# Part of a vector-matrix product moved from TensorE to ScalarE and GpSimd in a decoder layer

## The chip, the cores and the metric

The kernel runs on one core of a Trainium2 chip. The metric is the device time of one execution in microseconds (us), lower is better. Five engines work side by side, each in its own order: TensorE (PE; PEld is its weight load), VectorE (DVE), ScalarE (ACT), GpSimd (POOL) and SyncE (SP), which issues the transfers. [...]

## The reference

One post-norm decoder layer with D = 2048 and 1024 tokens. What matters here is its first part and one factor of its last:

```python
mod = c @ w_ada + b_ada                      # c (1, 2048), w_ada (2048, 6144)
shift, scale, gate = jnp.split(mod, 3, axis=-1)
h = _ln(x) * (1.0 + scale[:, None, :]) + shift[:, None, :]
proj = h @ w_in                              # (1024, 2048) by (2048, 9776), then the two mixers
...                                          # y: both mixers, merged and projected
x = _ln(ALPHA * x + gate[:, None, :] * y) * ln_g + ln_b
```

So `c @ w_ada` is a product of one vector with a matrix of 48 MB in float32; it has to be read once, and each weight is used once. Scale and shift are needed ahead of everything, the gate only at the end.

## The kernel before

A planner orders the instructions: the program is written in the order of the computation, and a timeline that the compiler works out ahead of the run fixes each engine's order. At run time an engine takes its instructions in that order and waits where one is not ready.

**First stage: scale and shift, and the first projection tiles.** x is loaded, normalised and transposed into 16 tiles xs[k] of 128 channels by 1024 tokens. Then the loop over k = 0, 2, ... 14 (eight rounds) makes scale and shift for two k at a time. In each round eight tiles wa of w_ss are loaded (512 KB each, `load_wa`, L150; they rotate through seven buffers, four of the pool p0 and three of the pool st, whose tag "stg" other stages share). A tile holds two chunks of 128 input channels by 512 columns. L187 multiplies each chunk on TensorE by the matching chunk of c, held in cP as 128x32 with c in the first column and zeros beside it. The 32 output rows of a chunk go to one of four groups of PSUM partitions of the bank mp, so four chunks are wanted at a time, and the bank sums over the loads. One float32 matmul shows as two rows in the trace, so one load as four. Then ScalarE copies mp to pm (L189), four matmuls with a column of ones sum over the partitions (L191), and VectorE adds the bias (L192, L193). With them VectorE scales and shifts xs[k] (L199), ScalarE rounds it (hhi, L201), VectorE takes the rest (hlo, L203), and `mm6` (L124, L125, L128) multiplies three projection tiles with three matmuls for each half of the tokens, 36 for two k. In between VectorE computes the tables of the state-space mixer (`Ssm.tables`, lines L1072 to L1148), which no one needs before the next stage. All loads go through SP's queue in one order.

**Second stage: dense tiles and blocks of the state-space mixer.** `dense` makes one projection tile: four weight units, each loaded (L109), rounded by ScalarE (whi, L111), its rest taken by VectorE (wlo, L113), and multiplied by `mm6`, 24 matmuls for a unit. Eight blocks of the mixer (`Ssm.block`) are laid between, two tiles to a block, three to the first. A block goes from TensorE (L1252 to L1274) to a long chain on VectorE (L1193, L1303) and back to TensorE (L1320, L1321). `gate_steps` is a generator that `dense` calls once for each unit. It computes the gate: for each of four blocks of 512 columns, eight loads wg of 512 KB in the tag "stg" (three buffers, which the evictions of the dense tiles use too), each with four chunks multiplied on TensorE as above (L365); after eight loads two copies by ScalarE (L370, L371), the load of the bias, one matmul with ones (L374) and an addition (L375).

Behind these come attention, the branches and the output projection, none of them touched. GpSimd has two uses in the kernel, both behind the second stage: a mask's addition in attention (L904) and the addition of ln_b in the last norm (L596).

Of the kernel before, what the change touches and what calls it, by code (L numbers as in the profile page):

```python
# [5 lines left out]
F32 = mybir.dt.float32  # L6
# [7 lines left out]
ADD, SUB, MUL, MAX, MIN = ALU.add, ALU.subtract, ALU.mult, ALU.max, ALU.min  # L14
# [16 lines left out]
def hybrid_kernel(tc, A, out):  # L31
    with ExitStack() as es:
        _hybrid(es, tc, A, out)
# [17 lines left out]
def _hybrid(es, tc, A, out):  # L51
    nc = tc.nc
    V, S, P, PE = nc.vector, nc.scalar, nc.gpsimd, nc.tensor
    ld, st_ = nc.sync.dma_start, nc.sync.dma_start
# [32 lines left out]
    cst = es.enter_context(tc.tile_pool(name="cst", bufs=1))  # L87
    ident = cst.tile([128, 128], F32, name="ident")
    ld(ident, A["ident"])
    ones = cst.tile([128, 128], F32, name="ones")  # L90
    V.memset(ones, 1.0)
    bada = cst.tile([128, KT, 2], F32, name="bada")
    ld(bada, A["bada"])
# [4 lines left out]
    stp = es.enter_context(tc.tile_pool(name="st", bufs=3))  # L98
# [5 lines left out]
    def w_unit(src, shape=[128, 4, 128], rp=None):  # L104

        raw = (rp or wp).tile([128, 512], F32, name="wraw", tag="wraw", bufs=3 if rp else WR)
        if len(shape) == 3:
            raw = raw.rearrange("p (k c) -> p k c", k=4)
        ld(raw, src)  # L109
        hi = wp.tile(shape, F32R, name="whi", tag="whi")  # L110
        S.copy(hi, raw)  # L111
        lo = wp.tile(shape, F32R, name="wlo", tag="wlo")
        V.tensor_tensor(lo, raw, f(hi), op=SUB)  # L113
        return hi, lo
# [15 lines left out]
    def stage(dt=F32):  # L130
        return stp.tile([128, T], dt, name="stg", tag="stg")
# [3 lines left out]
    cP = sc.tile([128, KT, 32], F32, name="cP")  # L135
# [5 lines left out]
    p0 = s0.enter_context(tc.tile_pool(name="p0", bufs=1))  # L141
# [2 lines left out]
    NS = 3  # L144
    units = []


    def load_wa(n):
        wa = (stp if n % 7 % 2 else p0).tile([128, 2, 512], F32, name="wa", tag="stg" if n % 7 % 2 else "wa", bufs=3 if n % 7 % 2 else 4)
        ld(wa, A["w_ss"][n // 8][:, 2 * (n % 8):2 * (n % 8) + 2])  # L150
        return wa

    xn, was = [], {}
    for b in range(NB):
        t = xh.tile([128, T], F32, name=f"xa{b}", tag="xh"), xh.tile([128, T], F32, name=f"xb{b}", tag="xh")
# [24 lines left out]

    for k in range(0, KT, 2):
        mp = pp.tile([128, 512], F32, name="mp", tag="mp", bufs=2)
        for n in range(8):
            wa = was.pop(4 * k + n) if 4 * k + n in was else load_wa(4 * k + n)
            for i in range(2):
                r = 32 * (2 * n % 4 + i)
                PE.matmul(mp[r:r + 32], cP[:, 2 * n + i], wa[:, i], start=n < 2, stop=n > 5, tile_position=(0, r))  # L187
        pm = p0.tile([128, 512], F32, name="pm", tag="pm", bufs=1)
        S.copy(pm, mp)  # L189
        for i in range(4):  # L190
            PE.matmul(mp[:, i:i + 1], pm[:, 128 * i:128 * i + 128], ones[:, :1], start=True, stop=True)  # L191
        V.tensor_tensor(mods[:, k:k + 2], mp[:, :4].rearrange("p (k i) -> p k i", k=2), bada[:, k:k + 2], op=ADD)  # L192
        V.tensor_scalar(mods[:, k:k + 2, 0:1], mods[:, k:k + 2, 0:1], 1.0, None, op0=ADD)  # L193
        if k % 4 == 0:
            units.append([w_unit(w_in[TILES["us"][i]][:, k:k + 4]) for i in range(NS)])

    acc = [[pp.tile([128, 512], F32, name="acc", tag="st", bufs=6) for _ in range(2)] for _ in range(NS)]
# [50 lines left out]
    def bank():  # L248
        return pss.tile([128, 512], F32, name="sps", tag="s")
# [103 lines left out]
    def gate_steps():  # L353

        for c in range(4):
            gp = bank()
            for hf in range(2):
                cs = slice(512 * c + 256 * hf, 512 * c + 256 * hf + 256)
                o = gp[:, 256 * hf:256 * hf + 256]
                for u in range(4):  # L360
                    wg = stp.tile([128, 4, 256], F32, name="wg", tag="stg")
                    ld(wg, A["w_gate"][4 * u:4 * u + 4, :, cs].rearrange("k p c -> p k c"))
                    for i in range(4):
                        r = 32 * i
                        PE.matmul(o[r:r + 32], cP[:, 4 * u + i], wg[:, i], start=u == 0, stop=u == 3, tile_position=(0, r))  # L365
                    yield
            cs = slice(512 * c, 512 * c + 512)
            s = stage()
            t, b = s[:, :512], s[0:32, 512:]
            S.copy(t, gp)  # L370
            S.copy(b, gp[0:32])  # L371
            ld(b, A["b_gate"][0:1, cs].to_broadcast([32, 512]))
            g2 = bank()
            PE.matmul(g2[0:32], ones[:, 0:32], t, start=True, stop=True)  # L374
            V.tensor_tensor(b, b, g2[0:32], op=ADD)  # L375
            st_(gate_d[:, cs], b[0:1])

# [25 lines left out]
    sp_cm = tc.tile_pool(name="sp", bufs=1)  # L403
    sp = sp_cm.__enter__()
    side = gate_steps()
    n = 0
    for b in range(8):
# [145 lines left out]
    with (tc.tile_pool(name="at2", bufs=1, side="right") as ap,  # L553
# [3 lines left out]
        def work():  # L557
            for i, t in enumerate(branch_nsa(psum_a, opd, 0)):
                st_(na_d[i], t)
                yield 1  # L560
            yield from glu(psum_a, (opd, opx), ap)
            yield from branch_ssm(psum_a, (opd, opx))

        w, n, grp = work(), 0, None
# [11 lines left out]
    mp = es.enter_context(tc.tile_pool(name="mp", bufs=32, side="right"))  # L576
# [74 lines left out]
    for c in range(4):  # L651
        cs = slice(512 * c, 512 * c + 512)
# [780 lines left out]
```

## Time and profile before

| | us |
|---|---|
| median of 3 runs | 3239.2 (3238.16 to 3239.89) |
| the profiled execution | 3234.84 |
| its span, first to last instruction | 3233.1 |
| TensorE busy | 3162.2 (98%) |
| VectorE busy | 1686.2 (52%) |
| ScalarE busy | 1127.2 (35%) |
| GpSimd busy | 85.5 (3%) |

The profile shows one execution. A window of it lists for each engine how long it was busy and how many instructions it had, the granted clock of TensorE (1.00 is 2.4 GHz) and the share of the DMA engines' time. The chain of waits is the work that ended last, followed back from the end; its shares by line tell which line the end waited for. A line of the timeline begins with an instruction's start and its duration, and in brackets stands how long the engine was idle ahead of it and for what. A busy TensorE need not be at its peak: a lone matmul on a quarter of the array is as busy as a full one.

### The profile page before, as it was taken

Reading aid. Unit: us, or ns where it says so; the run is one execution under the profiler, and the core shown is the slowest. Engines: PE = TensorE matmul, PEld = TensorE weight load, DVE = VectorE, ACT = ScalarE, POOL = GpSimd, SP = SyncE. Lnnn points to the kernel's source line nnn. Section 1 sums busy time; section 2 is a strip of 40 time slices with the busy share of each in tenths; the row PEclk is TensorE's granted clock in tenths of the full one; section 3 lists DMA queues with packets and bytes.
Section 4 is the critical chain, followed back from the end, with each engine's and each line's share of the span. In section 5 each row is a group of like instructions: output and inputs, shape, how many; then the busy total and the mean of one; then the engine's idle time right before and its main releaser. Section 6 shows DMA issues by size and latency. Waiting matters only on the chain.

```text
span 3233.1 us, 43112 instructions
## 1 busy us (share of the span) xinstructions
PE 3162.2 (98%) x15603; PEld 2538.1 (79%) x15603; DVE 1686.2 (52%) x4615; ACT 1127.2 (35%) x2327; POOL 85.5 (3%) x66
## 2 busy tenths in 40 slices
PE   7999999999999999999999999999999999999896
PEld 4467788888888888888888888887888888788784
DVE  8354678763444434334333334426777665534737
ACT  4212222222433334333433234325555443322323
POOL 0000000000000000000000000000000000000302
PEclk9999999999999999999999999999999999999998
DMA  9654524344322232222322222236668444734533
GB/s 335 236 170 147 172 94 141 103 128 119 117 92 74 77 97 88 71 64 83 97 77 74 67 84 91 76 126 202 213 207 285 142 131 147 241 114 144 166 119 138
DMA packets 286398, 432.21 MB, mean 134 GB/s; under 512 B 40324, under 2 KB 139428, under 8 KB 286184
## 3 DMA queue, kind: packets, MB, share of 16 engines
q1 hardware_dynamic: 286184, 429.45, 41.0%
q8 instruction: 123, 2.02, 0.3%
q14 instruction: 91, 0.75, 0.1%
HBM read 331.30 MB, written 98.05 MB: 133 GB/s over the span
## 4 chain that ended last, share of the span: by engine, by line
PE 93%; DVE 3%; DMA 2%; ACT 1%; issue 1%; SPq 0%; ACTq 0%; DVEq 0%
PE dps L124 17%; PE dps L125 17%; PE dps L128 17%; PE po L957 5%; PE ps L814 4%; PE pt L935 4%; PE pa L462 4%; PE pa L463 4%; PE pa L464 4%; PE e L602 2%; PE e L601 2%; PE e L603 2%; PE mp L187 2%; DVE r L595 1%; PE acc L124 1%; PE e L462 1%
## 5 line engine op out<-in xcount | busy, mean ns | idle before, releaser
L124 PE MATMUL dps<-hhi,whi 128*128 128x512 f32 x2336 | 927.8, 397 | 0.0
L125 PE MATMUL dps<-hlo,whi 128*128 128x512 f32 x2336 | 925.2, 396 | 0.0
L128 PE MATMUL dps<-hhi,wlo 128*128 128x512 f32 x2336 | 750.3, 396 | 0.0
L111 ACT CAST whi<-wraw 128x512 fp32r<-128x512 f32 x544 | 336.2, 619 | 1054.9 <-PE dps L125 622.7
L113 DVE TENSOR_TENSOR wlo<-wraw,whi 128x512 fp32r<-128x512 f32 x544 | 381.0, 701 | 600.9 <-ACT whi L111 587.8
L124 PEld LDWEIGHTS dps<-hhi,whi 128*128 128x128 f32 x2336 | 439.7, 188 | 103.8 <-issue 13.0
L125 PEld LDWEIGHTS dps<-hlo,whi 128*128 128x128 f32 x2336 | 439.8, 188 | 93.7 <-issue 7.0
L128 PEld LDWEIGHTS dps<-hhi,wlo 128*128 128x128 f32 x2336 | 433.4, 188 | 92.5 <-issue 5.7
L940 DVE TENSOR_TENSOR ptl<-pt,pth 128x512 fp32r<-128x512 f32 (+2 forms) x320 | 204.1, 646 | 269.3 <-ACT pth L939 267.6
L939 ACT CAST pth<-pt 128x512 fp32r<-128x512 f32 (+2 forms) x320 | 172.0, 552 | 456.7 <-PE pt L935 456.0
L462 PE MATMUL pa<-op,whi 128*128 128x512 f32 x528 | 210.0, 400 | 2.1 <-ACT op L449 1.7
L463 PE MATMUL pa<-op,whi 128*128 128x512 f32 x528 | 209.7, 397 | 2.5 <-DMA op<-oa_d 2.5
L464 PE MATMUL pa<-op,wlo 128*128 128x512 f32 x528 | 208.8, 396 | 0.0
L602 PE MATMUL e<-wlo,m 128*128 128x512 f32 x368 | 148.0, 402 | 9.9 <-DVE rsd L42 5.4
L603 PE MATMUL e<-whi,m 128*128 128x512 f32 x368 | 146.3, 398 | 0.0
L929 ACT ACTIVATE psl<-psl,mn 128x128 f32<-128x128 f32 (+7 forms) x128 | 99.2, 775 | 81.3 <-DVE mn L842 80.5
L601 PE MATMUL e<-whi,m 128*128 128x512 f32 x368 | 122.0, 401 | 0.6 <-ACT whi L111 0.6
L462 PEld LDWEIGHTS pa<-op,whi 128*128 128x128 f32 x528 | 99.8, 189 | 23.3 <-ACT op L449 3.3
L463 PEld LDWEIGHTS pa<-op,whi 128*128 128x128 f32 x528 | 99.6, 189 | 22.9 <-DMA op<-oa_d 2.9
L464 PEld LDWEIGHTS pa<-op,wlo 128*128 128x128 f32 x528 | 99.6, 189 | 20.1 <-issue 0.7
L904 POOL TENSOR_TENSOR near<-bn,msk 128x512 f32<-128x512 f32 x32 | 35.1, 1098 | 2662.1 <-DVE msk L900 2535.9
L883 ACT ACTIVATE pw<-pw,mn 128x640 f32<-128x640 f32 (+4 forms) x128 | 88.9, 694 | 32.4 <-DVE mn L842 31.6
(308 smaller groups left out, 4271.1 us busy)
## 6 DMA issues: line engine op xcount, KB each, us to landing
wraw<-in_w_in SPq DMA_DIRECT2D x304, 256.0 KB, 3.0
wraw<-in_w_out SPq DMA_DIRECT2D x136, 256.0 KB, 3.0
wa<-in_w_ss SPq DMA_DIRECT2D x64, 512.0 KB, 5.7
wg<-in_w_gate SPq DMA_DIRECT2D x32, 512.0 KB, 3.6
q<-q_d SPq DMA_DIRECT2D x64, 256.0 KB, 4.1
wraw<-in_w_bn SPq DMA_DIRECT2D x64, 256.0 KB, 3.1
q_d<-stg SPq DMA_DIRECT2D x32, 256.0 KB, 3.9
oa_d<-ptl SPq DMA_DIRECT2D x64, 128.0 KB, 2.2
```

The costliest lines, as they stand in the source:

```text
L111: S.copy(hi, raw)
L113: V.tensor_tensor(lo, raw, f(hi), op=SUB)
L124: PE.matmul(ps[hf], hi[:, ku], hhi[k][:, c], start=a, stop=False)
L125: PE.matmul(ps[hf], hi[:, ku], hlo[k][:, c], start=False, stop=False)
L128: PE.matmul(ps[hf], lo[:, ku], hhi[k][:, c], start=False, stop=z)
L462: PE.matmul(ps, hi[:, j], x[k][0], start=k == 0, stop=False)
L463: PE.matmul(ps, hi[:, j], x[k][1], start=False, stop=False)
L464: PE.matmul(ps, lo[:, j], x[k][0], start=False, stop=k == 7)
L601: PE.matmul(a, mk[0][:, t], hi, start=k == 0, stop=False)
L602: PE.matmul(a, mk[0][:, t], lo, start=False, stop=False)
L603: PE.matmul(a, mk[1][:, t], hi, start=False, stop=k == KT - 1)
L940: V.tensor_tensor(lo[0:n, :w], tp[0:n, :w], f(hi[0:n, :w]), op=SUB)
```

## The change

In the first stage, of the eight loads of a round the even ones go to TensorE as before, now with the other two groups of partitions for every second one. The odd ones go to ScalarE, which multiplies each chunk, partition by partition, with c as the scale of the instruction (`scaled_sum`, S.mul). The first odd tile of a round is written to an accumulator pa of 128x2x512; each later one is multiplied in place and added to pa by GpSimd (one addition of 128x1024). At the end of a round VectorE adds mp and the two halves of pa into pm, in the place of ScalarE's copy. In the second stage all of the gate's product goes that way: its loads are cut as 2 chunks by 512 columns instead of 4 by 256, ScalarE multiplies, GpSimd adds to gacc and adds the halves, and the one matmul with ones stays. The copy of the bank to SBUF goes, and the tile of ones shrinks.

```diff
-    ones = cst.tile([128, 128], F32, name="ones")
+    ones = cst.tile([128, 32], F32, name="ones")
...
+    def scaled_sum(acc, w, k, first):
+        for i in range(2):
+            S.mul((acc if first else w)[:, i], w[:, i], cP[:, k + i, 0:1])
+        if not first:
+            P.tensor_tensor(acc, acc, w, op=ADD)
...
         mp = pp.tile([128, 512], F32, name="mp", tag="mp", bufs=2)
+        pa = p0.tile([128, 2, 512], F32, name="pacc", tag="pacc", bufs=2)
         for n in range(8):
             wa = was.pop(4 * k + n) if 4 * k + n in was else load_wa(4 * k + n)
-            for i in range(2):
-                r = 32 * (2 * n % 4 + i)
-                PE.matmul(mp[r:r + 32], cP[:, 2 * n + i], wa[:, i], start=n < 2, stop=n > 5, tile_position=(0, r))
-        pm = p0.tile([128, 512], F32, name="pm", tag="pm", bufs=1)
-        S.copy(pm, mp)
+            if n % 2:
+                scaled_sum(pa, wa, 2 * n, n == 1)
+            else:
+                for i in range(2):
+                    r = 32 * (n % 4 + i)
+                    PE.matmul(mp[r:r + 32], cP[:, 2 * n + i], wa[:, i], start=n < 3, stop=n > 3, tile_position=(0, r))
+        pm = pa[:, 0]
+        V.tensor_tensor(pm, mp, pm, op=ADD)
+        V.tensor_tensor(pm, pm, pa[:, 1], op=ADD)
...
     def gate_steps():
         for c in range(4):
-            gp = bank()
-            for hf in range(2):
-                cs = slice(512 * c + 256 * hf, 512 * c + 256 * hf + 256)
-                o = gp[:, 256 * hf:256 * hf + 256]
-                for u in range(4):
-                    wg = stp.tile([128, 4, 256], F32, name="wg", tag="stg")
-                    ld(wg, A["w_gate"][4 * u:4 * u + 4, :, cs].rearrange("k p c -> p k c"))
-                    for i in range(4):
-                        r = 32 * i
-                        PE.matmul(o[r:r + 32], cP[:, 4 * u + i], wg[:, i], start=u == 0, stop=u == 3, tile_position=(0, r))
-                    yield
             cs = slice(512 * c, 512 * c + 512)
-            s = stage()
-            t, b = s[:, :512], s[0:32, 512:]
-            S.copy(t, gp)
-            S.copy(b, gp[0:32])
+            gacc = sp.tile([128, 2, 512], F32, name="gacc", tag="gacc")
+            for u in range(8):
+                wg = stp.tile([128, 2, 512], F32, name="wg", tag="stg")
+                ld(wg, A["w_gate"][2 * u:2 * u + 2, :, cs].rearrange("k p c -> p k c"))
+                scaled_sum(gacc, wg, 2 * u, u == 0)
+                yield
+            P.tensor_tensor(gacc[:, 0], gacc[:, 0], gacc[:, 1], op=ADD)
+            g2 = bank()
+            PE.matmul(g2[0:32], ones, gacc[:, 0], start=True, stop=True)
+            b = stage()[0:32, 512:]
+            S.copy(b, g2[0:32])
             ld(b, A["b_gate"][0:1, cs].to_broadcast([32, 512]))
-            g2 = bank()
-            PE.matmul(g2[0:32], ones[:, 0:32], t, start=True, stop=True)
             V.tensor_tensor(b, b, g2[0:32], op=ADD)
             st_(gate_d[:, cs], b[0:1])
```

## Rows read from the trace of the kernel before

**Rows 1.** The page: busy us of each engine, share of the span, instructions.
```profile
PE 3162.2 (98%) x15603; PEld 2538.1 (79%) x15603; DVE 1686.2 (52%) x4615; ACT 1127.2 (35%) x2327; POOL 85.5 (3%) x66
```

**Rows 2.** Windows: length; PE, PEld, DVE, ACT, POOL busy; clock, DMA share, GB/s.
```profile
15.00:45.00 30.00, 25.28 (x132) 14.47 (x133) 28.50 (x102) 22.10 (x39) 0.00 (x0) 0.89 0.97 372
...
45.00:105.00 60.00, 60.00 (x293) 30.66 (x293) 45.50 (x243) 19.22 (x30) 0.00 (x0) 1.00 0.89 308
105.00:177.00 72.00, 71.96 (x314) 39.13 (x313) 23.13 (x33) 16.24 (x23) 0.00 (x0) 1.00 0.53 178
...
212.00:271.40 59.40, 59.40 (x304) 42.58 (x297) 26.97 (x87) 8.46 (x15) 0.00 (x0) 1.00 0.51 162
271.40:331.40 60.00, 60.00 (x356) 44.07 (x354) 41.87 (x106) 14.41 (x25) 0.00 (x0) 1.00 0.50 153
```

**Rows 3.** Chain of waits by line, of 45 to 177 us and 212 to 430.
```profile
by line: PE mp L187 35.4%; PE acc L124 19.7%; PE acc L128 17.6%; PE acc L125 17.3%; PE mp L191 4.6%; PE tp L178 3.7%; ACT stg L214 1.0%; ACT whi L111 0.5%; issue 0.5%; ACTq L111 0.0%
...
by line: PE dps L124 27.7%; PE dps L125 25.8%; PE dps L128 25.7%; PE sps L365 8.0%; PE sps L1274 2.8%; PE sps L1320 2.7%; PE sps L1321 2.4%; PE sps L1252 1.4%; PE sps L374 1.3%; PE sps L1266 1.2%; PE sps L1256 0.8%
```

**Rows 4.** Window of 45 to 177 us, the instructions of L187 alone.
```profile
45.00:177.00 132.00, 49.77 (x220) 7.36 (x220) 1.00 0.70 237
```

**Rows 5.** Timeline of PE around one load's rows: start, us, line, count.
```profile
102.73 0.62 PE L128 MATMUL acc<-hhi,wlo 128*128 128x512 f32 x2
103.28 1.05 PE L187 MATMUL mp<-wa,cP 128*32 128x512 f32 x4
104.26 0.97 PE L124 MATMUL acc<-hhi,whi 128*128 128x512 f32 x3
```

**Rows 6.** Timeline of ACT: weight casts with the gate's work between, and without.
```profile
232.56 0.62 ACT L111 CAST whi<-wraw 128x512 fp32r<-128x512 f32 x1 [5.65 <-PE dps L125]
238.84 0.62 ACT L111 CAST whi<-wraw 128x512 fp32r<-128x512 f32 x1 [5.66 <-PE dps L125]
...
522.67 0.62 ACT L111 CAST whi<-wraw 128x512 fp32r<-128x512 f32 x1 [4.87 <-PE dps L125]
528.17 0.62 ACT L111 CAST whi<-wraw 128x512 fp32r<-128x512 f32 x1 [4.87 <-PE dps L125]
```

**Rows 7.** POOL's groups by line: count, busy us, mean ns of one, idle before.
```profile
L596 POOL TENSOR_TENSOR r<-r,ln_b 128x512 f32<-128x512 f32 x30 | 50.2, 1702 | 480.5 <-DVE r L595 474.8 <-issue 5.7
L904 POOL TENSOR_TENSOR near<-bn,msk 128x512 f32<-128x512 f32 x32 | 35.1, 1098 | 2662.1 <-DVE msk L900 2535.9 <-DVE mn L842 126.2
```

**Rows 8.** Timeline of POOL and DVE at two places.
```profile
1043.47 1.05 POOL L904 TENSOR_TENSOR near<-bn,msk 128x512 f32<-128x512 f32 x1 [1043.03 <-DVE msk L900]
...
1043.80 1.27 DVE L113 TENSOR_TENSOR wlo<-wraw,whi 128x512 fp32r<-128x512 f32 x1 [0.46 <-ACT whi L111]
...
3219.08 2.86 POOL L596 TENSOR_TENSOR r<-r,ln_b 128x512 f32<-128x512 f32 x2 [0.63 <-DVE r L595]
...
3221.22 0.74 DVE L45 SCALAR_TENSOR_TENSOR rsd<-rsd 128x1 f32<-128x1 f32 x1 [0.33 <-ACT rsd L44]
```

**Rows 9.** ACT's groups by line: a multiplication with a scale from memory.
```profile
L981 ACT ACTIVATE pw<-pw,gsc 128x512 f32<-128x512 f32 x16 | 10.7, 715 | 2.5 <-DVE gsc L978 2.5
```

**Rows 10.** Timeline: end of a block's chain on DVE, and its use on PE.
```profile
355.12 1.41 DVE L1193 TENSOR_TENSOR e<-t,t 64x512 f32<-64x512 f32 x2
...
359.80 0.38 PE L1321 MATMUL sps<-e,v 128*128 128x127 f32 x2
```

**Rows 11.** Timeline of PE between the stages.
```profile
178.82 4.03 PE L348 MATMUL sps<-oh,rbx 32*128 32x384 f32 x8 [1.86 <-ACT stg L214]
...
183.80 0.63 PE L124 MATMUL dps<-hhi,whi 128*128 128x512 f32 x1
...
187.66 0.39 PE L124 MATMUL dps<-hhi,whi 128*128 128x512 f32 x1
```

**Rows 12.** Waits of SP's queue, 0 to 240 us: total, times, longest.
```profile
SPq L150 <- PE mp L187: 77.0, 41, 5.1
```

**Rows 13.** DVE's groups by line in 45 to 177 us.
```profile
L113 DVE TENSOR_TENSOR wlo<-wraw,whi 128x512 fp32r<-128x512 f32 x12 | 8.3, 690 | 31.7 <-ACT whi L111 30.8 <-PE acc L128 0.9
```

## The prediction

> **What bounds the kernel now.** I read the page's engine shares first: TensorE is busy for 98% of the span and GpSimd for 3% [rows 1]. A change that moves work off TensorE can therefore pay, but only in the stretch where TensorE is last, so next come the two stretches that the diff touches, cut into windows [rows 2], and the shares of the chain of waits inside each [rows 3]. What to see: from 45 to 177 us TensorE is busy without a gap, and 35.4% of the chain is the scale and shift matvec (L187); from 212 to 430 us it is busy without a gap again, and 8.0% of the chain is the gate's matvec (L365). Then look at the other engines in the same rows. VectorE is busy 45.5 of 60 us in 45 to 105, 23.1 of 72 in 105 to 177, and 41.9 of 60 in the block from 271.4. ScalarE is under a third busy from 45 us on, GpSimd idle. Last, the queue of waits of SP: the weight loads of L150 wait for TensorE to free their buffers, 77.0 us in all [rows 12], so memory follows TensorE in this stretch. Its own floor lies below what follows: 89% of the DMA engines' time is taken in 45 to 105, 53% behind.
>
> **Part 1, scale and shift: what TensorE gives up.** In 45 to 177 us 220 matmul rows stand under L187, that is 55 loads' worth (four rows each), busy 49.8 us [rows 4]. Seen singly: the projection's matmuls before it have a pitch of 0.23 us and would go on at 103.19; after one load's four rows the next three run from 104.26 and end at 105.23, which is what three would do that began at 104.37 [rows 5]. So a lone load costs 1.18 us. Several together cost less. From the shares: 46.7 us of L187, and 72.1 us for the 288 matmuls of the projection that would take 65.8 us at 0.2285 (24 of them in 5.49 us [rows 6]), so 6.3 us more for restarts: 53 us for 55 loads, 0.96 each. Afterwards only even loads go to TensorE: 32 in all, of which I put 5 ahead of 45 us (of the 9 that lie there now), so 27 at 0.96 to 1.18 = 26 to 32 us. Freed: 21 to 27 us, I take 24. TensorE would need 108 us of the 132.
>
> **What part 1 adds.** ScalarE: 64 multiplications of 128x512 with a scale from memory. The nearest row is L981 at 0.715 us [rows 9]: 46 us, less the eight copies of L189. From 45 us on it is busy for 35 of 132 [rows 2], so it has the room. But each waits for its load, and behind it in ScalarE's order stand the casts that feed the projection (L201, L111). I count nothing here, with up to 1.4 us (one pair) for each of 8 rounds as the price if a load is late.
> GpSimd: 3 additions of 128x1024 in each of 8 rounds, 24. Its two kinds of 128x512 addition take 1.10 and 1.70 us in the mean [rows 7]; a 128x1024 is an estimate of 2.1 us (twice the 1.05 of the single one in rows 8) to 3.4. I take 2.1, since the 1.70 holds waiting time, as the next paragraph shows: 50 us.
> VectorE: two additions in each round, 16 additions of 128x512; L113, of that size, takes 0.69 [rows 13]: 11 us. The first of the two waits for GpSimd's last addition of the round; behind it in VectorE's order stand L199, L203 and L113, and TensorE waits for these.
> SP: an odd load's buffer comes free when GpSimd is done, some 4 us later than now, and all loads behind the next one into it wait with it. Seven buffers hold 3.7 MB, 12 us at the 308 GB/s of 45 to 105 [rows 2], so I count nothing; without that cover it would be 4 us a round.
>
> **What GpSimd takes from VectorE.** This decides the case. At 1043.80 a split of L113 starts beside a GpSimd addition that began at 1043.47 and ends at 1044.52 [rows 8]; it takes 1.27 us where 0.69 is usual, so it did nothing until the addition was over. A VectorE instruction of one element (L45) that starts at 3221.22 takes 0.74 us and ends just behind a GpSimd pair that ends at 3221.94 [rows 8]. And GpSimd's 1.70 in the last stage would be 1.05 plus some 0.65 for which VectorE held it. I read it so: where VectorE's instruction takes two operands from SBUF, the two engines take turns, a whole instruction each.
> So the 50 us of additions are up to 50 us taken from VectorE. Its need from 45 to 177 would be 68.6 + 11 + 50 = 130 us if all of it falls on VectorE's work, against TensorE's 108. If it all falls into idle time, 80 us. VectorE's idle time now lies almost all behind 105 us; ahead of it the tables' many small operations (L1072) fill the gaps, and they read two tiles. I take 80% ahead of 105 us and 60% behind: 0.7 x 50 = 35, so 115 us, a gain of 17 if it were packed without gaps. It is not: VectorE's order is laid out ahead of time, the small operations stand ahead of the scaling of x (L199) and the split (L203), and TensorE's next round waits for those. I take half of it, 8 us, with bounds from 0 to 24.
>
> [...]
>
> **The start.** From 15 to 45 us VectorE is busy 28.5 of 30 and ScalarE 22.1, while TensorE has idle time [rows 2]; the first round's matvec is free there now. It would put 8 x 0.715 = 5.7 us on ScalarE and 3 x 2.1 + 1.4 = 7.7 us on VectorE's turn. Bounds 0 and 8 us; I take 3, since the first round can wait a little for x anyway. Part 1 together: 8 - 3 = 5 us gained, from -8 to 24.
>
> **Part 2, the gate.** One visit to TensorE: with it ScalarE's cast of a weight unit recurs each 6.28 us, without it each 5.49 us [rows 6]; a unit is 24 matmuls of 0.2285. A visit costs 0.79, 32 cost 25.3 us. That is all taken away; the sum over partitions stays (L374), and one copy for each of four columns (L370) goes from ScalarE. The loads are as many and as large. Added: 64 multiplications on ScalarE (46 us, which is busy 14 of 60 us in a block: hidden), 28 GpSimd additions of 2.1 and 4 of 1.05, 63 us. Each load now keeps its "stg" buffer until GpSimd is done, some 4 us longer; it shares three buffers with the evictions, and a load that waits for one holds the weight loads (L109) behind it on SP. Two units of weights stand ahead, 11 us, which covers it: nothing.
> VectorE: a block is 60.0 us with 41.9 busy and would be 53.7 on TensorE's account [rows 2]. With 7 x 2.1 + 1.05 = 15.8 us of additions VectorE would need up to 57.7. So each of the three blocks gains 2.3 to 6.3 us; the stretch ahead of them, 27.0 of 59.4 busy, gains its 6.3 in full. 13 to 25 us. Against that, VectorE's chain from the rotation to the product ends 3.3 us ahead of TensorE's use (356.53 against 359.80) [rows 10]; two additions in it are 4.2 us, and every block may stall for 1 to 3 us. I take 18, from 4 to 25.
>
> **Sum.** 5 + 18 = 23. The profiled execution is 3234.8 us, 1.7 of them outside its span of 3233.1, and would become 3211.8. It lies 4.4 us below the median of the runs, 3239.2, against which the result counts: 3216 us.
>
> **Rivals.** (a) The additions mostly find VectorE idle or reading PSUM: 24 + 25 less 3 to 5 = 45 us gained, 3194. For it: VectorE has 63 us idle in 132 and 18 in 60. Against: the idle time lies where it waits for TensorE, and not where it is needed. (b) VectorE is the bound: part 1 gives -3 (130 for 132, less the start), the gate 6 to 13: 3239 - 6 = 3233, no change. (c) Slower: TensorE, starved while VectorE is held, loses its clock. After 1.9 us idle and a few matmuls on 32 rows the projection's matmuls run at 1.2 GHz until 187 us, 0.63 instead of 0.39 each [rows 11]; 512 columns at that clock are a pitch of 0.427 for 0.2285. A round has 36 of them, so 7.1 us more; in the five rounds that the tables would reach into, if their 22 us (45.5 less four rounds of 5.8) go in at 4 to 5 us a round, 35 us: 3251. It decides from waits of some 2 us a round on; a round takes 5.8 us on VectorE now (23.1 for the four in 105 to 177) and would take 5.8 + 1.4 + 6.3 = 13.5, as long as on TensorE, so every small operation laid between comes on top and such waits can come. Against: the matvec's own matmuls lie between. (d) The change doesn't do what it says: the matvec stays as long on TensorE because even loads come singly; then 55 loads at 0.96 become 27 at 1.18, which is in the bounds above and still leaves 21: part of the forecast.
>
> **How the numbers follow.** Forecast 0.47 at 3216, (a) 0.20, (b) 0.16, (c) 0.17. A measurement of this kernel tells some 0.2% (6.5 us) from no change. Faster by more: forecast, (a) and a little of (b) = 0.69; within: the rest of (b), 0.14; slower: 0.17. The range takes in (a) and (b), and stops ahead of (c): 3192 to 3244.
>
> **What would show it.** Right: no matmul under the gate's load, units at 5.5 us from 212 to 430 with GpSimd some 63 us busy, and VectorE's additions near 1.3 to 2.7 us where GpSimd runs. The projection of the first stage should end at 166 to 176 instead of 177 us, with VectorE, not TensorE, as the releaser. Wrong: splits that keep 0.69 us beside GpSimd (then a), or a granted clock below 0.95 between 45 and 150 us with longer gaps on TensorE (then c); a GpSimd addition over 2.5 us without VectorE beside it would push it towards (b).

## The result, and the profile after

The changed kernel takes 3275.8 us (median of 4 runs) where the kernel before, run beside it, takes 3238.7: ratio 1.0115, 95% interval 1.0101 to 1.0130. The forecast was 3216, a gain of 23 us; it is a loss of 37. Line numbers of after are 7 to 14 higher: L187 is now L199, L199 is L212 (x), L203 is L216 (hlo), L191 to L192 are L204 to L205, and the mixer's L1193 is L1200; the multiplication by ScalarE is L150, GpSimd's addition L152.

First the engines on the page of after, in the columns of [rows 1]:

```profile
PE 3153.0 (96%) x15219; PEld 2543.9 (78%) x15219; DVE 1784.4 (55%) x4631; ACT 1201.5 (37%) x2443; POOL 227.5 (7%) x122
```

TensorE lost 384 instructions as the diff says and has only 9 us less busy time; VectorE is busy for 98 us more, though its new work is 16 additions. The windows of after, in the columns of [rows 2], say where:

```profile
15.00:45.00 30.00, 20.06 (x96) 10.88 (x96) 28.65 (x76) 22.01 (x39) 5.97 (x3) 0.85 0.97 370
45.00:105.00 60.00, 46.70 (x198) 28.82 (x198) 57.72 (x214) 32.30 (x52) 22.88 (x9) 0.82 0.71 245
105.00:177.00 72.00, 62.74 (x250) 36.31 (x250) 55.70 (x98) 33.86 (x51) 32.69 (x13) 0.93 0.65 219
212.00:300.00 88.00, 84.79 (x375) 61.24 (x373) 51.54 (x110) 27.35 (x47) 27.86 (x12) 0.98 0.49 155
300.00:400.00 100.00, 91.00 (x442) 72.17 (x443) 87.85 (x160) 34.23 (x58) 30.87 (x13) 0.97 0.46 146
400.00:500.00 100.00, 94.42 (x493) 75.83 (x492) 83.71 (x188) 31.29 (x53) 20.32 (x8) 0.97 0.37 122
```

Where TensorE had no gap [rows 2] it now idles 13.3 us of 60 and 9.3 of 72, at a granted clock of 0.82 and 0.93 (at 0.50 part of the time: in 80.5 to 83.5 us, just behind a wait of 7.40 us for hlo, the matmuls start 0.427 us apart, against 0.234 in 92.5 to 94.8); VectorE is all but full in 45 to 105 (57.7 us of 60). In 212 to 500, the gate's stretch, TensorE idles 17.8 us.

To place the loss, ScalarE's instructions that both traces have under the same tiles were matched, and the median taken of how much later they start in after, by their time in before:

```
before, us      160-320  320-480  480-640  640-800  800-960  1280-1440  1920-2080  end
after, later by   18.9     23.9     26.9     29.2     31.3      36.4       43.4    39.6
```

A first loss is there by the end of the first stage: its evictions (ScalarE's copies of the finished tiles out of PSUM) start at 194.10 instead of 175.24. The first of them in before; that of after stands with the experiment adds_on_vector:

```profile
175.24 1.07 ACT L214 COPY stg<-acc 128x512 f32<-128x512 f32 x2
```

A second loss goes on growing: behind 560 us it is some 1.1 us in each 100 us as far as 2080 us, where the diff touches nothing. The casts of weight units show it: between the two of each pair lie the same seven units. The timeline of ScalarE, first of before, then of the kernel ones_small, of which the next section tells:

```profile
1008.94 0.62 ACT L111 CAST whi<-wraw 128x512 fp32r<-128x512 f32 x1 [1.48 <-PE dps L125]
...
1055.75 0.62 ACT L111 CAST whi<-wraw 128x512 fp32r<-128x512 f32 x1 [0.81 <-PE dps L125]
```

```profile
1017.98 0.62 ACT L111 CAST whi<-wraw 128x512 fp32r<-128x512 f32 x1 [1.54 <-PE dps L125]
...
1065.32 0.62 ACT L111 CAST whi<-wraw 128x512 fp32r<-128x512 f32 x1 [0.82 <-PE dps L125]
```

46.81 us against 47.34, with TensorE without a gap in both. Taken over all pairs of consecutive matmuls of the projection (some 6,000 rows each), the mean from start to start ("pitch" below) is 229.7 ns in before and 233.5 in after; in the last stage's rotations (e from whi or wlo, and m) it is 233.5 in before and 229.1 in after, the other way round.

### The profile page after: what moved, and what is told of

It is laid out like the page before. It is cut to its first block, busy times and chain, and to the rows that moved or that the text cites. A ratio compares the mean times of both kernels' runs of the same rounds, so it can differ in the third digit from the quotient of the medians.

```text
span 3272.6 us, 42677 instructions
## 1 busy us (share of the span) xinstructions
PE 3153.0 (96%) x15219; PEld 2543.9 (78%) x15219; DVE 1784.4 (55%) x4631; ACT 1201.5 (37%) x2443; POOL 227.5 (7%) x122
## 4 chain that ended last, share of the span: by engine, by line
PE 84%; DVE 8%; DMA 3%; issue 2%; ACT 2%; SPq 0%; POOL 0%; ACTq 0%; DVEq 0%; POOLq 0%
PE dps L124 15%; PE dps L128 15%; PE dps L125 15%; PE po L964 4%; PE ps L821 4%; PE pt L942 4%; PE pa L470 3%; PE pa L471 3%; PE pa L469 3%; PE e L609 2%; PE e L608 2%; PE e L610 2%; DVE r L602 1%; DVE wlo L113 1%; DVE t L1200 1%
```

## Experiments: the place of the buffers

The one thing in the diff that reaches so far is the first line: `ones` is 32 wide instead of 128. No step of the prediction names it. Everything allocated behind it on the left side of SBUF lies 384 bytes lower; the projection's moving operands, on the right side, stay.

**ones_small**: before with that line alone.

```
-    ones = cst.tile([128, 128], F32, name="ones")
+    ones = cst.tile([128, 32], F32, name="ones")
```

> The kernel before with one thing of the change alone: the tile of ones is 32 wide and no longer 128, so that every tile allocated behind it on the left side of SBUF lies 384 bytes lower. No work changes. In the trace of after the projection's matmuls (L124, L125, L128) follow each other at 233.5 ns where before had 229.7, and those of the later rotations (e from whi and m) at 229 where before had 233.5. Theory of the place: the addresses do that; then this kernel shows the same two figures and takes some 7000 x 3.9 ns less 900 x 4.5 ns = 23 us more than before, about 3255 to 3262 us, and stage one still ends at 175 us. Rival, another chip or another run of it: 229.7 and 233.5 as before, and 3239 us.

Measured: 3256.5 us, ratio 1.0057 (1.0044 to 1.0071), so 18.7 us lost with no change in work; pitch 233.5 ns and 229; evictions at 175.57. The theory of the place holds.

**after_old_place**: after with `ones` 128 wide (and 18 of the tables' small buffers for 20, to make room).

> After with ones 128 wide again, as in before, so that the buffers of weights lie where they lie in before; to make room the tables' small buffers are 18 in place of 20. Theory of the place: pitch of the projection's matmuls 229.7 ns and not 233.5, 18 to 20 us less than after: 3256 to 3258 us. Rival, the small ones cost time in before's order only: 3276 us.

Measured: 3256.4 us; pitch 229.7. The 19 us are in after and come off there too. Matched with before as in the table above, its instructions start 18.1 us later in 160 to 320, 21.4 in 320 to 480, and 21.4 still in 1920 to 2080: the loss that grew was the place's alone.

**pitch_by_place**: TensorE alone, with the two operands moved step by step; the core of it:

```
for n in range(12):
    for h in range(4):
        PE.matmul(ps[h % 2], w[:, wo + 128 * (n % 4):wo + 128 * (n % 4) + 128],
                  m[:, mo + 512 * (h % 2):mo + 512 * (h % 2) + 512], start=n == 0 and h < 2, stop=n == 11 and h > 1)
...
for i in range(32):
    group("w" + letters(i), 8 * i, 0)
for i in range(32):
    group("m" + letters(i), 0, 8 * i)
```

> No part of the reference is computed: x is copied to the output, and TensorE runs 64 groups of 48 fp32r matmuls of 128x128 by 128x512, each weight slice used four times, once with the weights and once with the moving operand placed 32 bytes further in each group; nothing else reads or writes SBUF. In the kernels the projection has weights at 416 bytes and the moving operand at 480 (modulo 512) where its pitch is 229.7 ns, and 32 and 480 where it is 233.5; the rotation has 480 and 416 at 233.5, 480 and 32 at 229. Theory that the distance of the two places decides (448 fast, 64 slow, modulo 512): in both sweeps the pitch follows the distance, about 229 at 448 and 233.5 at 64. Rival, the place of the one or the other by itself: one sweep is flat. Rival, it needs other engines' or transfers' access beside it: both sweeps are flat.

Timeline of TensorE, the first matmul of ten groups; from one to the next the weights lie 32 bytes further (the first at distance 0), and there are 48 matmuls between two rows:

```profile
88.96 0.39 PE L69 MATMUL pxwaa<-m,w 128*128 128x512 f32 x1
99.85 0.39 PE L69 MATMUL pxwab<-m,w 128*128 128x512 f32 x1
111.04 0.40 PE L69 MATMUL pxwac<-m,w 128*128 128x512 f32 x1
122.24 0.39 PE L69 MATMUL pxwad<-m,w 128*128 128x512 f32 x1
133.48 0.39 PE L69 MATMUL pxwba<-m,w 128*128 128x512 f32 x1
144.63 0.40 PE L69 MATMUL pxwbb<-m,w 128*128 128x512 f32 x1
155.84 0.40 PE L69 MATMUL pxwbc<-m,w 128*128 128x512 f32 x1
166.83 0.40 PE L69 MATMUL pxwbd<-m,w 128*128 128x512 f32 x1
178.03 0.39 PE L69 MATMUL pxwca<-m,w 128*128 128x512 f32 x1
188.91 0.39 PE L69 MATMUL pxwcb<-m,w 128*128 128x512 f32 x1
```

The groups take 10.89 us at distance 0, 11.15 to 11.24 at 32 to 160, 10.99 at 192, 11.20 at 224, and 10.88 again at 256. The pattern repeats every 256 bytes through all 32 groups, and moving the other operand instead gives the mirror image (229.1 ns where it lies 64 further on, 233.4 where the weights do). So it is the distance, place of the weights less place of the moving operand, modulo 256, and no other engine has to be at work for it: 226.7 ns at 0, 229.0 at 192, 232 to 234 elsewhere. In before the projection stands at 192 and the rotations, where the weight buffers are the moving operand, at 64; 384 bytes turn the one into the other.

**before_aligned**: 64 unused bytes ahead of the weight buffers, which puts both at distance 0.

```
+    pad = cst.tile([128, 16], F32, name="pad")
+    V.memset(pad, 0.0)
```

> The kernel before with an unused tile of 64 bytes per partition ahead of the weight buffers: the split weights then lie at 224 modulo 256, as the projection's moving operands and the rotations' other operand do (in before: 160, a distance of 192). Theory of the distance, from the bare stream of matmuls (226.7 ns at distance 0, 229.0 at 192, 233.4 at 64): the projection's pitch falls from 229.7 to 226.7 and the rotations' from 233.5 to about 227; 7000 x 3.0 + 1440 x 6.5 ns = 30 us, 3208 us. Rival, what the bare stream shows is covered in the kernel by other limits (the split, the evictions, or a different neighbour of the moved buffers): 3225 to 3240 us.

Measured: 3218.3 us, ratio 0.9947 (0.9935 to 0.9960): 17 us gained, not 30. The rotations run at 227.0 as expected, the projection at 228.5 and not 226.7. That the distance decides in the whole kernel too is shown by a pitch that neither kernel had. The gain lies between the two forecasts (3208, and 3225 to 3240), since the projection fell by 1.2 ns and not by 3; what keeps it 1.8 ns above the bare stream is open.

## Experiments: the parts, and where the additions are

**ss_only** and **gate_only** each take one half of the change (ss_only with `ones` 32 wide, gate_only with 128).

> The change in scale and shift alone, with ones 32 wide; the gate is on TensorE as before. Theory of turns: the 24 additions hold VectorE while the tables' small operations are in its order, so the first stage's evictions start at about 194 us as in after (175 before), and the kernel costs 19 us over the kernel with small ones: 3275 to 3280 us if addresses cost 23 us, 3258 if they cost nothing. Rival, the loss of stage one comes from the gate's presence (buffers, order): evictions at 175, no cost over small ones.

> The change in the gate alone, ones 128 wide as before, so that the addresses of weights and buffers are those of before. Theory of turns: the 25 us that TensorE is spared are given back by waits for VectorE in the mixer's blocks; between the end of stage one and 700 us the loss is the 2 to 3 us that remain in after when the slower matmuls (1600 x 3.9 ns = 6 us) are taken off: 3238 to 3244 us. Theory of the place alone: the gate's gain is hidden in after behind the slower matmuls and the start; then the gate alone gains its 18 us of the forecast: 3221 us.

Measured: ss_only 3275.7, 19 us over ones_small, evictions at 192.48, as expected; gate_only 3247.1, 9 over before, which is more than either theory had. On top of ss_only the gate's half adds nothing (3275.8). So of the 37 us some 19 are the place, 19 the first stage, and the gate, which was to gain 18, gives between 0 and a loss of 9. The halves do not add up exactly; the orders in which the instructions are laid out differ, but that this is the reason was not shown.

**adds_on_vector**: after with every addition on VectorE.

```
-            P.tensor_tensor(acc, acc, w, op=ADD)
+            V.tensor_tensor(acc, acc, w, op=ADD)
```

> After with all additions of the products on VectorE in place of GpSimd (28 + 24 of 128x1024 and 4 of 128x512), nothing else. An addition there should take 1.3 to 1.4 us (twice L113's 0.69) for GpSimd's 2.36 to 2.6. Theory of turns: what hurts is the time that VectorE loses, and it loses only 1.3 instead of up to 2.6 each, 73 us in all instead of 136: the first stage ends some 8 us earlier than in after (186), the mixer loses less, 3255 to 3268 us. Rival, ScalarE's order (multiplications that wait for loads or for their accumulator stand ahead of its casts): no change to after, 3276, evictions at 194.

Measured: 3226.4 us, with the place of after. The first evictions on ScalarE's timeline in after, then in adds_on_vector, and the additions among DVE's groups there:

```profile
194.10 1.07 ACT L227 COPY stg<-acc 128x512 f32<-128x512 f32 x2
```

```profile
162.25 1.06 ACT L227 COPY stg<-acc 128x512 f32<-128x512 f32 x2
```

```profile
L152 DVE TENSOR_TENSOR gacc<-gacc,wg 128x1024 f32<-128x1024 f32 x28 | 34.2, 1222 | 24.3 <-ACT wg L150 23.1 <-ACT gacc L150 1.0
L152 DVE TENSOR_TENSOR pacc<-pacc,wa 128x1024 f32<-128x1024 f32 x24 | 29.2, 1217 | 1.6 <-ACT wa L150 1.0 <-DMA wa<-in_w_ss 0.6
```

The first stage ends 32 us earlier than in after and 13 earlier than in before; an addition takes VectorE 1.22 us. The direction was expected, the size was not: 29 us of VectorE's own work in the first stage cost next to nothing.

What happens in after. POOL's groups of after, in the columns of [rows 7]:

```profile
L152 POOL TENSOR_TENSOR gacc<-gacc,wg 128x1024 f32<-128x1024 f32 x28 | 72.9, 2604 | 179.7 <-ACT wg L150 120.0 <-ACT gacc L150 56.4 <-DMA wg<-in_w_gate 2.3
L152 POOL TENSOR_TENSOR pacc<-pacc,wa 128x1024 f32<-128x1024 f32 x24 | 62.8, 2620 | 115.0 <-ACT wa L150 95.7 <-ACT rsd L44 6.6 <-DVE ss L1079 4.5
```

And the timeline of POOL (two rows) and of DVE beside it, while VectorE computes the mixer's tables:

```profile
65.25 2.41 POOL L152 TENSOR_TENSOR pacc<-pacc,wa 128x1024 f32<-128x1024 f32 x1 [4.52 <-DVE ss L1079]
70.53 8.07 POOL L152 TENSOR_TENSOR pacc<-pacc,wa 128x1024 f32<-128x1024 f32 x3 [2.87 <-ACT wa L150]
```

```profile
65.32 2.38 DVE L1079 TENSOR_TENSOR ss<-ss,ss 128x32 f32<-128x32 f32 x1
67.63 0.18 DVE L1079 TENSOR_TENSOR ss<-ss,ssi 128x32 f32<-128x32 f32 x1
...
70.91 2.43 DVE L1155 COPY rv<-pw 128x32 f32<-128x32 f32 x1
...
73.73 2.51 DVE L1079 TENSOR_TENSOR sst<-pw 128x32 f32<-128x32 f32 x2
76.16 2.51 DVE L1079 TENSOR_TENSOR sst<-pw,pw 128x32 f32<-128x32 f32 x2
```

An operation of 0.19 us becomes one of 2.4: VectorE stands still for the whole addition. A copy, with one operand, is held as well (L1155 at 70.91: 2.43 us for 0.19), and so is a scaling (L1087 at 58.40: 2.37 us for 0.17). Not held is an instruction that has one of its two operands in PSUM: the eight of 128x512 in after that began inside an addition (mp plus pacc, L201, and sps times rot, L1200) took 0.67 to 0.69 us, their usual time. The mixer shows both kinds side by side, POOL and then DVE:

```profile
299.65 5.13 POOL L152 TENSOR_TENSOR gacc<-gacc,wg 128x1024 f32<-128x1024 f32 x2 [8.32 <-ACT wg L150]
```

```profile
302.47 1.27 DVE L1200 TENSOR_TENSOR t<-sps,rot 128x512 f32<-128x512 f32 x2
303.78 1.55 DVE L1200 TENSOR_TENSOR e<-t,t 128x512 f32<-128x512 f32 x1
```

The two products with sps in PSUM run at 0.68 each; the next, with both operands in SBUF, ends behind the addition. The held time is reckoned so: summed over VectorE's instructions that overlap an addition, what each took above the lower quartile of its line and size is 93 us in after, 45 of them in the first stage; the tables' 240 operations take 74.2 us instead of 46.5.

**no_adds**: the additions of 128x1024 left out.

> After without the additions on GpSimd (the four of 128x512 at the ends of the gate's columns stay); ScalarE's multiplications, loads, buffers and VectorE's sums stay. Left out of the result: the odd loads behind the first, and the gate's behind the first. Theory of turns: what is left has no cost on VectorE but 11 us, evictions at 157 to 163 us, at or a little under those with the additions on VectorE (162.3), and 3205 to 3222 us with ones 32 wide. Rival, ScalarE's order (multiplications ahead of its casts): a good part of the loss stays, evictions behind 175 us.

Measured: 3217.1 us, evictions at 160.91. ScalarE's 128 multiplications in its order are no cost by themselves. In after some of them also wait for an accumulator, 13.4 and 7.6 us, and those waits are gone here together with the additions; what the longer one costs is read in the trace of after, ScalarE and then VectorE:

```profile
86.93 1.33 ACT L150 ACTIVATE pacc<-wa,cP 128x512 f32<-128x512 f32 x2 [13.40 <-PE mp L204]
88.27 2.00 ACT L214 CAST hhi<-x 128x1024 fp32r<-128x1024 f32 x2
```

```profile
87.37 1.53 DVE L212 TENSOR_SCALAR x<-x,mods 128x1024 f32<-128x1024 f32 x2
```

The cast behind the multiplications needs the x that VectorE has ready at 88.18 (the first of the two, 0.81 us), so the wait held it up by 0.1 us; behind the wait of 7.6 us the casts wait another 2.2 for x. That rival falls.

**adds_aside**, **aside_one_source** and **one_source_in_chain** ask whether VectorE is held, or only waits for GpSimd's sum. Each replaces GpSimd's addition by:

```
 adds_aside            P.tensor_tensor(w, w, w, op=ADD)
 aside_one_source      P.tensor_scalar(w, w, 2.0, None, op0=MUL)
 one_source_in_chain   P.tensor_scalar(acc, w, 2.0, None, op0=MUL)
```

> After, but each GpSimd addition of 128x1024 adds the scaled load to itself, in its own buffer, in place of adding it to the accumulator; the sums over the odd loads behind the first, and the gate's behind the first, are left out of the result. GpSimd does as many instructions of the same size with two reads from SBUF and holds the load's buffer as long, but VectorE's sum (L201) no longer waits for them. Theory of turns: VectorE is still held for up to 2.4 us by each, the splits and small operations beside them take 1.3 to 2.5 us, and the first stage's evictions start at 185 to 194 us (after: 194.1, before: 175.2); 3262 to 3276 us. Rival, the latency of GpSimd's chain (three additions of 2.4 us in a row, and VectorE's sum standing in its order for the last): evictions at 160 to 172 as with the additions on VectorE (162.3), and 3225 to 3245 us.

> The same kernel as adds_aside with one thing changed: GpSimd's instruction on the scaled load is a multiplication by 2 (one read from SBUF and one write) in place of an addition (two reads). Left out of the result: the same sums. Theory of turns, in the narrow form (two engines with two reads from SBUF each exclude each other): a split beside it keeps its 0.69 us, evictions 160 to 172, below 3245 us. In the wide form (any GpSimd instruction of this size holds VectorE): as adds_aside. Theory of the chain's latency: as adds_aside, at 160 to 172 both.

> After, but GpSimd writes twice the scaled load into the accumulator in place of adding it: one read from SBUF, the same accumulator, the same waits for the multiplication before and of VectorE's sum behind. Left out of the result: the sums over the odd loads but the last. In aside_one_source such an instruction took GpSimd 2.9 us, longer than the addition (2.62), and held VectorE for 43 us in all where after has 93. Theory of turns: VectorE runs beside it, evictions of the first stage near 170 us as there (169.8), and 3231 to 3240 us. Theory of the chain's latency (VectorE's sum waits for GpSimd's last result): evictions at 185 or later, since each link is longer than in after, 3260 us and more.

Measured, with the held time found as above in the first stage (not for the additions that are VectorE's own):

```
                      GpSimd, ns each  held, us  evictions   us
after                 2620             45        194.1       3275.8
adds_aside            2243             31        179.6       3250.4
one_source_in_chain   3135             22        171.0       3236.0
aside_one_source      2927             24        169.8       3230.7
no_adds               -                 0        160.9       3217.1
adds_on_vector        (VectorE 1217)    -        162.3       3226.4
```

The evictions follow the held time, to some 2 us, and not GpSimd's time. one_source_in_chain has the longest chain and all of its waits, and is 23 us earlier than after; against aside_one_source the waits cost 1.2 us. adds_aside missed its window from below: its additions are shorter and hold less, which fits, but that nothing else is in the difference was not tested. GpSimd also keeps the loads' buffers longer, but that is not what costs: in aside_one_source it keeps them for 2.9 us where after has 2.6, and in after the loads waited for GpSimd 8.7 us in all in the first stage, 3.2 at most. How one source holds less is seen in aside_one_source, POOL and then DVE:

```profile
62.35 2.82 POOL L152 TENSOR_SCALAR wa<-wa 128x1024 f32<-128x1024 f32 x1 [4.47 <-ACT wa L150]
```

```profile
62.47 1.02 DVE L1085 TENSOR_SCALAR pw<-ss 128x32 f32<-128x32 f32 x1
63.39 0.28 DVE L1079 TENSOR_TENSOR ss<-ss,ss 128x32 f32<-128x32 f32 x2
63.59 0.33 DVE L1079 TENSOR_TENSOR sst<-pw 128x32 f32<-128x32 f32 x2
```

VectorE stands for the first 1.0 us of GpSimd's 2.8 and goes on at its usual pace beside the rest.

**tables_late** and **tables_late_vector**: the tables' pool is opened only when the first stage's has closed, with the additions on GpSimd and on VectorE.

```
+    s0.close()
     sct_cm = tc.tile_pool(name="sct", bufs=1)
     sct = sct_cm.__enter__()
     ssm.tables(sct)
```

> After, but the tables' buffers are taken only when the first stage has given up its own, so that the mixer's 240 small operations on VectorE run behind the first stage and none stands between its scalings and splits. GpSimd's additions stay. In after GpSimd held VectorE for 45 us up to 212 us, most of it on these small operations (74.2 us for 46.5 in before), and the evictions started at 194. Theory that the additions hurt through the small operations standing in VectorE's order: evictions at 160 to 172; what that gives back is lost again in part behind it, where the first mixer block waits for the tables. Rival, the additions hurt the projection directly (its splits and sums held, at 2.4 us each): evictions at 182 to 194 all the same.

> As tables_late with the additions on VectorE. Both theories: evictions at 155 to 163 us (162.3 with the tables in between). The difference to tables_late is what GpSimd's additions cost the projection without the tables: 0 to 10 us by the first theory, 20 to 30 by the rival.

Measured: evictions at 175.87 and 161.44 (3282.5 and 3237.2 us; both lose time behind it, which was not followed up). tables_late lies between the two forecasts, and so does the difference of the pair. With the tables between, GpSimd's additions cost 31.8 us over VectorE's; without, 14.4. Both theories had a share: 17 us of the loss go through the tables' small operations, which stand in VectorE's order ahead of what TensorE needs, and 14 fall on the projection's own steps. That adding 29 us of VectorE's own work costs 1 us because the order is laid out with it in mind, and GpSimd's hold is not, fits this (with VectorE's additions 39 of the 240 small operations are behind 130 us, in after 14) but was only argued.

**vector_old_place** and **vector_aligned** put the findings together: additions on VectorE, the place as before, and the place at distance 0.

> Additions on VectorE as in adds_on_vector (3226.4 us), with ones 128 wide and 18 small buffers, so that both losses found are gone. Theory of the place and of turns together: 3226 - 19 = 3207 us, first stage's evictions at 162 us, pitch 229.7 ns, about 1% faster than before. Rival, the two do not add up (VectorE or a load becomes the bound once the matmuls are quicker): 3215 to 3226.

> Additions on VectorE as in adds_on_vector (3226.4 us) and the weights at 224 modulo 256 (ones 32 wide, an unused tile of 192 bytes, 19 small buffers of the tables). Theory of the distance: as vector_old_place (3207.5) less the same 30 us: 3178 us, 1.9% faster than before. Rival, with quicker matmuls VectorE or the loads become the bound where the additions are: in the first stage and the mixer part of it is lost, 3185 to 3195 us.

Measured: 3207.5 us, ratio 0.9908 (0.9892 to 0.9923), and 3188.8 us, ratio 0.9857 (0.9842 to 0.9872). Both beat both kernels. The first is as summed. By the ratios the second gains 16.5 us more, what the distance gave in before (17), and not the 30 of the bare stream. It lies in its rival's range, but the same shortfall in before_aligned, where VectorE has no additions, speaks against that rival.

## Why the prediction was wrong, step by step

- What TensorE gives up was right: 128 rows of the matvec instead of 256, none under the gate's loads. ScalarE's 0.715 us was 0.716, and it hid, as said.
- GpSimd's addition was mis-sized: 2.1 us taken, 2.35 to 2.41 where it did not wait for VectorE (65.25 above), 2.6 in the mean; 142 us for all 56 instructions instead of 113.
- The turns, a whole instruction each, were the right mechanism but drawn too narrow: copies and scalings with one operand are held too (2.43 us for the copy at 70.91, 2.37 for the scaling at 58.40). A whole instruction is right for the addition (2.38 us of VectorE beside 2.41 of GpSimd, at 65.25), and not for GpSimd's one-source instruction, where 1.0 us of 2.8 was held.
- The held share, 0.7, was right: 45 of 62.8 us; only the longer additions made 45 of the 35 forecast, which moves the sum by 10. Even VectorE's need came out, 113.4 us busy in 45 to 177 (57.72 + 55.70) for 115. The step that failed is the next one, "I take half of it": VectorE's need was set against TensorE's, 115 us against 132, and part of the rest called a gain. What is late counts in its place, not in the sum: the holds fell on 0.2-us operations that stand ahead of the scaling and the split, TensorE waited, and its granted clock fell to a mean of 0.82 and 0.93 in the two windows.
- That was rival (c), given 0.17, with the sign and the mark named for it (clock below 0.95 between 45 and 150 us, longer gaps). Its 1.2 GHz is, in the trace of before, a granted clock of 0.50 (183 to 187 us), where matmuls of 512 columns start 0.427 us apart: 1.2 columns a ns, an estimate from that pitch, by which 1.00 would be 2.4. It put the whole price on the clock, 35 us; the trace has more in the waits themselves. Stage one by its terms: 22.6 us idle in 45 to 177; 10.8 + 5.0 us lost to the clock (0.18 of 60, 0.07 of 72), some 4 of them while TensorE was idle anyway; 5.2 us less done ahead of 45; less the 24 freed: 16 to 20 against the 19 measured.
- The start was put at 3 us and cost 8.4 (the first L192 at 45.63, L205 at 54.04), a little over its upper bound of 8.
- The gate's gain of 18 was taken as VectorE's room less a stall of 1 to 3 us a block. 48 us of hold fell on the mixer's chain. Timeline of DVE at a block's start, beside two additions from 307.40 to 312.29:

```profile
306.57 3.53 DVE L1310 TENSOR_TENSOR_SCAN et<-rho,e 128x128 f32<-128x128 f32 x4
310.02 2.82 DVE L1200 TENSOR_TENSOR e<-t,t 128x512 f32<-128x512 f32 x1
```

  Such a 128x512 product takes 0.69 without, four scans 1.36. From 212 to 500 us TensorE idles 17.8 us and loses some 8 to its clock: 25.6, as much as the 25.3 that the visits gave. That the additions are the cause is shown by the time from the first eviction to the end, in the profiled executions, all with the place of after: ones_small, with the gate on TensorE, 3081.0; after 3080.3; adds_aside 3071.8; one_source_in_chain 3065.0; adds_on_vector 3064.1; aside_one_source 3060.9; no_adds 3056.8. The gate gains 24 us without the additions, what the visits cost; 17 with them on VectorE, near the 18 forecast; and 1 with them on GpSimd.
- A line was not costed at all: `ones` narrower by 384 bytes, 19 us. No term and no rival of the sum could hold it.
- A slip without effect: in rival (b), 132 less 130 less a start of 3 is a loss of 1, not of 3.

The sum: a gain of 23 forecast, a loss of 37 measured, 60 us apart: 19 the place, 24 the first stage (a gain of 5 forecast, a loss of 19), 17 or a little more the gate.

## What to carry to other kernels

Time that a second engine takes from a busy one is not priced by that engine's free time but by what stands next in its order; before moving work to GpSimd, try the same instruction on VectorE, which was twice as quick here (1.22 us for 2.35 to 2.6). Cost every line of a diff that moves an allocation: in a kernel bound by fp32r matmuls like these, try weights and moving operand at the same place modulo 256 bytes (17 us of 3235 gained in before_aligned), and look at the pitch of the matmuls before and after.

## What the runs showed of the hardware

- In pitch_by_place, with TensorE alone, 512-column fp32r matmuls follow each other at 226.7 ns where the weights' and the moving operand's places are equal modulo 256 bytes, at 229.0 at a distance of 192, and at 232 to 234 at the others tried (multiples of 32).
- In after, a GpSimd addition of a 128x1024 load to the accumulator, both in SBUF, takes 2.35 to 2.41 us where it did not wait, and stops VectorE for all of it (2.38 us for an operation of 0.19), a copy (2.43 for 0.19) or a scaling (2.37 for 0.17) with one source too, but not the eight 128x512 VectorE instructions with one of their two operands in PSUM (0.67 to 0.69 us beside it, as without); in adds_on_vector VectorE does that addition in 1.22. In aside_one_source a one-source instruction of the same size takes GpSimd 2.8 us and stops VectorE for about 1.0.
